# The S5 constants inside the first SwiGLU of a decoder block: whole pieces, part on VectorE, late zero stores, block sums in one tile per pair of rows

## The chip, the cores and the metric

The kernel runs on one core of a Trainium2 chip. The metric is the time of one execution in microseconds (us) of device time; the number that stands for a kernel is the median of its runs.

## What is computed

The reference is one layer of a decoder: half a SwiGLU, a mixer that joins sparse attention (8 heads) with an S5 state space layer, half a second SwiGLU, a gated per-layer input. The sequence has 512 rows, the model is 1024 wide, the hidden layer 2816 wide, everything in float32. The parts that matter here:

```python
h = h + 0.5 * swiglu(rmsnorm(h, norm_ffn1[i]), ffn1_w1[i], ffn1_w3[i], ffn1_w2[i])
z = rmsnorm(h, norm_mix[i]) @ w_in[i]
...
lam = lax.complex(a_re.astype(f32), a_im.astype(f32))
dt = jnp.exp(log_dt.astype(f32))[:, None]
a_bar = jnp.exp(lam * dt)
b_coef = (a_bar - 1.0) / lam
...
_, state = lax.associative_scan(combine, (a_seq, bu), axis=1)
```

The S5 layer has 32 groups of 16 channels with 64 complex states each. Its constants depend on the parameters alone (powers of `a_bar`, their products with the input and output matrices, cosines and sines), so the kernel can work them out while the first SwiGLU runs.

## The kernel before

**The first SwiGLU.** The hidden layer is cut into 22 tiles of 128 columns ("ups" 0 to 21), in four chunks of 6, 6, 5 and 5; after a chunk's ups comes its "down", which multiplies the chunk's hidden tiles back and adds to h. The first up of the next chunk stands ahead of each down. So up 12 is followed by down 1, then come ups 13 to 17, down 2, ups 18 to 21 and down 3. Each float32 product is made of three TensorE (PE) matmuls in a reduced float32 type: ScalarE (ACT) rounds a weight tile to `hi` (L164), VectorE (DVE) makes the rest `lo` (L166), and PE takes hi*hi, hi*lo and lo*hi. Weights come in units of 128x1024 (512 KB) through a ring of four buffers `raw`. Ups 0 to 13 use PSUM banks A and B and one 512-wide pass for each product; from up 14 on (`PLAIN`), `up_fast` forms a block product with seven instead of eight multiplications, for which DVE makes sums of weights (`s13`, `s24`, L342 to L351) and sums of the input.

**Sums of the input.** `renorm(k)` runs inside down 1, after every second of its eight output rows. It loads rows k and k+4 of x again (`xr`, L416, on SyncE's queue), scales them, splits them into xh and xl (L418 to L420), and makes the four sums of quarters in a tile `xt` (L427 to L430), which is split into `sh` and `sl` (L431, L432). Before, `sh` and `sl` are one tile each for all four k; `xt` shares its place with `s13` and `s24` by turns. These tiles lie where the S5 constants' pool was; a tile there has to wait until everything that used the place is done. In memory, `xt` of before overlaps `gt`.

**The S5 constants.** `s5_constants` is a generator: `ffn` takes the next piece of it behind an up, and `yield n` says that the next piece is not to come before up n. What is in a `with paced()` waits on GpSimd (POOL) for a small copy `step` that DVE makes at the end of each up (L407); POOL copies it to `seen` (L558). In order the generator makes: small tables on DVE; `ft`, eight times three POOL operations (L707 to L709); 32 transposes of it on PE (L715), copied to `fs` and stored to DRAM; `gt`, nine times three POOL operations (L728 multiply, L729 multiply into `ct`, L730 subtract), which takes the place of `ft` and so waits for the transposes; three stores of `gt` to DRAM (L731, L733); `kt`, 32 small matmuls of `b2` by `gt` (PE, bank D), eight stores of it interleaved with seven stores of zeros from the tile `zz` (L754); tables of cosines and sines `tcs` by doubling, j = 0 to 5 (L773 to L779), a multiply by a sign (L782) and two stores.

The instructions of each engine stand in one fixed list, in-order; a scheduler writes the lists at build time from the order of the code and its own estimates, apart from those that are pinned. An instruction that waits holds everything behind it on its engine. POOL, SyncE and ACT issue the DMAs.

Of the kernel before, what the change touches and what calls it, by code (L numbers as in the profile page):

```python
# [10 lines left out]
F32 = mybir.dt.float32  # L11
# [18 lines left out]
NG = 32  # L30
# [46 lines left out]
def block_kernel(ctx: ExitStack, tc: tile.TileContext, a: dict, out: bass.AP):  # L77
# [104 lines left out]
    class Norm:  # L182
# [25 lines left out]
        def quarter(self, r, c):  # L208
            ks, cs = slice(4 * r, 4 * r + 4), slice(256 * c, 256 * c + 256)
            return self.xh[:, ks, cs], self.xl[:, ks, cs]  # L210

# [5 lines left out]
    class Scaled(Norm):  # L217
# [13 lines left out]
        def spread(self, tmp, xpool, pool, pb):  # L231
# [22 lines left out]
            def combine(n, a, b, op):  # L254
                t = tmp().rearrange("p a (b c) -> p (a b) c", c=256)
                with tc.issue_after(self.last.ins):
                    for i in range(2):
                        V.tensor_tensor(t[:, 2 * i:2 * i + 2], a(i), b(i), op)
                hi = pool.tile([128, 4, 256], FR, name=f"sh{n}")
                lo = pool.tile([128, 4, 256], FR, name=f"sl{n}")  # L260
                S.copy(hi, t)
                V.tensor_tensor(lo, t, hi.bitcast(F32), OP.subtract)
                return (hi, lo), lambda i: t[:, 2 * i:2 * i + 2]

            q = {(r, c): (lambda i, r=r, c=c: quarter(r, c, i)) for r in range(2) for c in range(2)}
            self.t1, t1 = combine(1, q[0, 0], q[0, 1], OP.subtract)
            self.t2, t2 = combine(2, q[1, 1], t1, OP.add)
            self.t4, _ = combine(4, q[1, 0], t2, OP.subtract)
            self.t3, _ = combine(3, q[0, 1], q[1, 1], OP.subtract)

# [45 lines left out]
    def ffn(nrm, done, pools, plain, bg=None, first=None):  # L316
        wait = next(bg) if bg else None
        fast = bg is None
        with ExitStack() as fctx:
# [13 lines left out]
            def up_fast(f):  # L333
# [10 lines left out]
                u1 = split(s13.rearrange("p b c -> p (b c)"), kept=made.append)  # L344
                ah, al = (xp.tile([128, 512], FR, tag=n, name=n) for n in ("ah", "al"))
                with tc.issue_after(made[0].ins):
# [11 lines left out]
                def product(o, w, half, x, first):  # L358
                    for k in range(4):
                        sl = slice(512 * half + k * 128, 512 * half + (k + 1) * 128)  # L360
                        for i, (a_, b_) in enumerate(((0, 0), (0, 1), (1, 0))):
                            mm(o, w[a_][:, sl], x[b_][:, k], first and k + i == 0, k == 3 and i == 2,
                               skip_group_check=True)
# [22 lines left out]
                product(zx[:, lo], (ah, al), 0, nrm.quarter(1, 0), False)  # L386
                product(zy[:, lo], u2, 0, nrm.t2, False)
                product(zz[:, lo], u2, 1, nrm.quarter(1, 1), False)
# [20 lines left out]
            def renorm(k):  # L409
# [17 lines left out]
                V.tensor_tensor(t[:, 0], xs[0][:, c[0]], xs[0][:, c[1]], OP.subtract)  # L427
                V.tensor_tensor(t[:, 1], xs[1][:, c[1]], t[:, 0], OP.add)
                V.tensor_tensor(t[:, 2], xs[0][:, c[1]], xs[1][:, c[1]], OP.subtract)
# [122 lines left out]
    def s5_constants(sp, late_pool):  # L552
        yield 3
        if True:
# [157 lines left out]
            for g in range(0, NG, 4):  # L712
                p = bank("D")
                for j in range(4):
                    PE.transpose(p[:, j * 128:(j + 1) * 128], ft[:, g + j].rearrange("p s i -> p (s i)"), ident)  # L715
# [9 lines left out]
            for k in range(9):  # L725
                yield 8 + k // 3
                with paced():
                    G.tensor_tensor(gt[:, :, k, :], cp, bc(pr[:, k]), OP.mult)  # L728
                    G.tensor_tensor(ct, cx[:, 1], bc(pi[:, k]), OP.mult)  # L729
# [7 lines left out]
            for g in range(0, NG, 16):  # L737
# [12 lines left out]
            zz = late_pool.tile([128, 1, 112], F32, tag="zz", name="zz")  # L750
            G.memset(zz, 0.0)
# [28 lines left out]
            nc.gpsimd.dma_start(cd, tc_)  # L780
            for g in range(0, NG, 8):
                G.tensor_scalar(ts_[:, g:g + 8], ts_[:, g:g + 8], pos, None, OP.mult)  # L782
            nc.gpsimd.dma_start(sd, ts_)
# [22 lines left out]
    with ExitStack() as f1:  # L806
# [926 lines left out]
```

## Time and profile before

| | before |
|---|---|
| runs | 1086.9, 1090.21, 1092.48 us (median 1090.21) |
| profiled execution | 1088.84 us, span 1087.0 us |
| granted TensorE clock, mean | 0.987 |
| PE busy | 1040.2 us (96%) |
| DVE busy | 823.3 us (76%) |
| ACT, POOL busy | 492.0 us, 172.0 us |
| moved by DMA | 135.19 MB, 26.4 + 8.4 + 6.6% of the 16 engines' time |

"Busy" is time in which an engine has an instruction in work. A view of windows gives this for stretches of the span; in it, (x) counts instructions and PEclk is the share of TensorE's full clock that the chip granted there. A view of waits lists who waited for whom, as "waiter <- the one waited for: total us, times, longest us". The chain is the path followed back from the last instruction, each piece as "start, length, what". Groups give "busy us, mean ns of one". The end of a wait tells which dependency came last, and not what else would have come soon after. The first SwiGLU takes about the first 390 us of the span.

### The profile page before, as it was taken

The page shows a single profiled execution, that of the slowest core. Times are in us where ns is not written, and L with a number is a line of the kernel's source. Part 1 is how long each engine was busy: PE and PEld are TensorE (multiplying, and loading weights), DVE is VectorE, ACT ScalarE, POOL GpSimd, SP SyncE. Part 2 cuts the span into 40 slices and gives each one's busy share as a digit, 9 for nine tenths or more (in the row PEclk, how much of TensorE's full clock was granted, in tenths as well). Part 3 has the DMA queues.
Part 4 walks back from the last instruction along what each step waited for, and adds up shares of the span by engine and source line. Part 5 has one row for each costly group of instructions (what it writes and reads, how often), then busy time and mean ns, then how long its engine had stood idle before and what let it go on. Part 6 is the DMA issues. An engine that isn't in the chain of part 4 may idle for free.

```text
span 1087.0 us, 15732 instructions
## 1 busy us (share of the span) xinstructions
PE 1040.2 (96%) x6057; PEld 881.5 (81%) x6057; DVE 823.3 (76%) x1371; ACT 492.0 (45%) x852; POOL 172.0 (16%) x187
## 2 busy tenths in 40 slices
PE   8999999776998999998899999999999999999997
PEld 5887888665987988876668668899899899899886
DVE  5699456747978876788579887998589669677766
ACT  6322233313633553235677884655255345344542
POOL 2004648913059110010000000000000000000001
PEclk9999999888999999999999999999999999999999
DMA  7432325493434574876631003333333333323322
GB/s 249 158 97 97 97 82 183 122 190 106 122 111 115 145 248 127 226 253 185 187 118 59 1 21 125 107 117 117 97 98 117 100 94 117 97 97 117 106 88 78
DMA packets 52939, 135.19 MB, mean 124 GB/s; under 512 B 10817, under 2 KB 19105, under 8 KB 52865
## 3 DMA queue, kind: packets, MB, share of 16 engines
q10 hardware_dynamic: 26352, 90.77, 26.4%
q0 software_dynamic: 6416, 22.12, 8.4%
q1 hardware_dynamic: 20096, 21.31, 6.6%
q8 instruction: 47, 0.77, 0.3%
q14 instruction: 28, 0.22, 0.1%
HBM read 116.19 MB, written 17.83 MB: 123 GB/s over the span
## 4 chain that ended last, share of the span: by engine, by line
PE 75%; DVE 8%; DMA 7%; POOL 3%; issue 3%; ACT 2%; SPq 0%; ACTq 0%; DVEq 0%; POOLq 0%
PE ps_A L133 22%; PE ps_C L133 20%; PE ps_B L133 18%; PE ps_D L133 14%; DMA s5o<-gt 2%; DVE lo L166 2%; DMA xr<-in_xT 1%; POOL ct L729 1%; POOL gt L730 1%; DMA qf<-qd 1%; DMA qd<-r 1%; DMA h<-in_xT 1%; DMA kcd<-ra 1%; DVE h L525 0%; DVE el L1344 0%
## 5 line engine op out<-in xcount | busy, mean ns | idle before, releaser
L164 ACT CAST hi<-raw 128x1024 fp32r<-128x1024 f32 (+2 forms) x143 | 144.5, 1010 | 262.2 <-PE ps_C L133 96.3
L133 PE MATMUL ps_C<-hq,hi 128*128 128x512 f32 x704 | 217.9, 391 | 1.5 <-DVE h L525 1.3
L166 DVE TENSOR_TENSOR lo<-raw,hi 128x1024 fp32r<-128x1024 f32 (+2 forms) x143 | 179.7, 1258 | 43.7 <-ACT hi L164 42.7
L133 PEld LDWEIGHTS ps_C<-hq,hi 128*128 128x128 f32 x704 | 131.5, 189 | 29.6 <-ACT hi L164 1.7
L133 PE MATMUL ps_C<-hq,lo 128*128 128x512 f32 x352 | 136.8, 390 | 0.0
L133 PE MATMUL ps_A<-xh,hi 128*128 128x512 f32 (+1 forms) x352 | 126.6, 360 | 8.8 <-ACT xh L419 5.8
L133 PE MATMUL ps_A<-xh,lo 128*128 128x512 f32 (+1 forms) x352 | 124.1, 356 | 11.2 <-DVE lo L166 11.2
L133 PE MATMUL ps_A<-xl,hi 128*128 128x512 f32 (+1 forms) x352 | 125.7, 357 | 1.4 <-DVE xl L420 1.2
L164 ACT CAST hi<-s 128x1024 fp32r<-128x1024 f32 x56 | 59.0, 1053 | 99.2 <-PE ps_D L133 51.3
L166 DVE TENSOR_TENSOR lo<-s,hi 128x1024 fp32r<-128x1024 f32 x56 | 71.8, 1281 | 18.1 <-ACT hi L164 17.7
L133 PEld LDWEIGHTS ps_A<-xh,lo 128*128 128x128 f32 x352 | 67.6, 192 | 20.9 <-DVE lo L166 12.0
L133 PEld LDWEIGHTS ps_A<-xh,hi 128*128 128x128 f32 x352 | 67.5, 192 | 19.9 <-ACT xh L419 6.2
L133 PEld LDWEIGHTS ps_A<-xl,hi 128*128 128x128 f32 x352 | 67.4, 192 | 12.5 <-DVE xl L420 1.9
L133 PEld LDWEIGHTS ps_C<-hq,lo 128*128 128x128 f32 x352 | 66.2, 188 | 13.9
L525 DVE SCALAR_TENSOR_TENSOR h<-ps_C,h 128x512 f32<-128x512 f32 x64 | 43.9, 687 | 37.8 <-PE ps_C L133 37.5
L133 PE MATMUL ps_B<-sh,hi 128*128 128x256 f32 x224 | 63.1, 282 | 0.7 <-ACT hi L164 0.7
L133 PE MATMUL ps_B<-sh,lo 128*128 128x256 f32 x224 | 63.1, 282 | 0.6 <-DVE lo L166 0.6
L133 PE MATMUL ps_B<-xh,hi 128*128 128x512 f32 (+1 forms) x168 | 63.4, 378 | 0.0
L133 PE MATMUL ps_D<-sl,hi 128*128 128x256 f32 x224 | 63.0, 281 | 0.0
L133 PE MATMUL ps_B<-sl,hi 128*128 128x256 f32 x224 | 62.9, 281 | 0.0
L133 PE MATMUL ps_D<-sh,hi 128*128 128x256 f32 x224 | 62.8, 280 | 0.0
L133 PE MATMUL ps_D<-sh,lo 128*128 128x256 f32 x224 | 62.7, 280 | 0.0
(439 smaller groups left out, 2498.6 us busy)
## 6 DMA issues: line engine op xcount, KB each, us to landing
raw<-in_wpack ACTq DMA_DIRECT2D x168, 512.0 KB, 3.6
so<-s5o POOLq DMA_DIRECT2D x8, 768.0 KB, 6.0
si<-s5i POOLq DMA_DIRECT2D x8, 512.0 KB, 5.0
h<-in_xT SPq DMA_DIRECT2D x8, 256.0 KB, 4.7
s5i<-fs POOLq DMA_DIRECT2D x1, 2048.0 KB, 12.4
xr<-in_xT SPq DMA_DIRECT2D x8, 256.0 KB, 6.8
s5o<-gt POOLq DMA_DIRECT2D x1, 2048.0 KB, 13.1
s5o<-gt POOLq DMA_DIRECT2D x2, 1024.0 KB, 19.7
```

What stands on the lines that cost most here:

```text
L133: return PE.matmul(o, lhsT, rhs, start=start, stop=stop, **kw)
L164: p, q = S.copy(hi[:, c], raw[:, c]), None
L166: q = V.tensor_tensor(lo[:, c], raw[:, c], hi[:, c].bitcast(F32), OP.subtract)
L525: V.scalar_tensor_tensor(h[:, m, :], o[m], 0.5, h[:, m, :], OP.mult, OP.add)
L729: G.tensor_tensor(ct, cx[:, 1], bc(pi[:, k]), OP.mult)
L730: G.tensor_tensor(gt[:, :, k, :], gt[:, :, k, :], ct, OP.subtract)
```

## The change

1. The generator's pieces are larger: `ft` comes in two halves behind ups 5 and 6, all transposes and copies to `fs` in one piece behind up 7, `gt` in three pieces of three k behind ups 8, 9 and 10.
2. Of gt's nine first multiplies, six (k over 2) go to DVE, three stay on POOL.
3. The memset of `zz` and its seven stores stand ahead of `ft` and wait for a `step`; in before's lists, POOL issues them at the program's start.
4. `dd` takes the tag of `bt` and `ct`, so DVE's write of `dd` waits for POOL's last use of `ct`.
5. `yield 13` stands ahead of kt's eight stores, and each waits for a `step`, that of up 13. The tables j = 0 to 3 follow in the same piece, j = 4 and 5 from up 17 on.
6. `xt` goes to the pool of the sums under the tag `aa`, which `ah` and `al` also share as one tile later; `sh` and `sl` are one tile for each k. Of these, only the pair for k = 3 lies where `gt` lies; `s13` and `s24` lie there too.
7. The sign is put into six columns of `sn` by one small DVE operation ahead of the tables, in place of four POOL operations of 128x512 behind them.

```diff
             ft = sp.tile([128, NG, 8, 16], F32, tag="big0", name="ft")
             for s_ in range(8):
-                yield 5 + s_ // 4
+                if s_ % 4 == 0:
+                    yield 5 + s_ // 4
...
                 S.copy(fs[:, g:g + 4].rearrange("p g n -> p (g n)"), p)
-                if g % 8 == 4:
-                    yield 7 + g // 16
...
             for k in range(9):
-                yield 8 + k // 3
+                if k % 3 == 0:
+                    yield 8 + k // 3
+                if k > 2:
+                    V.tensor_tensor(gt[:, :, k, :], cp, bc(pr[:, k]), OP.mult)
                 with paced():
-                    G.tensor_tensor(gt[:, :, k, :], cp, bc(pr[:, k]), OP.mult)
+                    if k < 3:
+                        G.tensor_tensor(gt[:, :, k, :], cp, bc(pr[:, k]), OP.mult)
...
-            dd = sp.tile([16, NG, 16], F32, name="dd")
+            dd = sp.tile([16, NG, 16], F32, tag="bt", name="dd")
...
+            yield 13
             for s_ in range(8):
-                w = 128 - 16 * s_
-                nc.gpsimd.dma_start(md[16 * s_:16 * s_ + 16, :, 16 * s_:], kt[:, :, :w])
-                if s_:
-                    nc.gpsimd.dma_start(md[16 * s_:16 * s_ + 16, :, :16 * s_], zz[16 * s_:16 * s_ + 16, :, :16 * s_].to_broadcast([16, NG, 16 * s_]))
+                with paced():
+                    nc.gpsimd.dma_start(md[16 * s_:16 * s_ + 16, :, 16 * s_:], kt[:, :, :128 - 16 * s_])
...
+            snp = sn[:, 3:9]
+            V.tensor_scalar(snp, snp, pos, None, OP.mult)
             for j in range(6):
-                if j > 2:
+                if j > 3:
                     yield 17
...
-            for g in range(0, NG, 8):
-                G.tensor_scalar(ts_[:, g:g + 8], ts_[:, g:g + 8], pos, None, OP.mult)
...
-                if not k:
-                    nrm.ts = [xp.tile([128, 4, 4, 256], FR, name=n) for n in ("sh", "sl")]
-                    for i in range(4):
-                        setattr(nrm, f"t{i + 1}", tuple(t[:, :, i] for t in nrm.ts))
-                t = cp.tile([128, 4, 256], F32, tag=("s13", "s24")[k % 2], name="xt", bufs=1)
+                t = xp.tile([128, 4, 256], F32, tag="aa", name="xt")
+                sums = [xp.tile([128, 4, 256], FR, name=f"{n}{k}") for n in ("sh", "sl")]
+                for i in range(4):
+                    nrm.t[i].append([x[:, i] for x in sums])
```

In POOL's list, the stretch of `gt` from its middle to its end reads so before:

```order
L728 TENSOR_TENSOR gt<-cp,pr 128x32x16
L729 TENSOR_TENSOR ct<-cx,pi 128x512
L558 COPY seen<-step 128x1
L728 TENSOR_TENSOR gt<-cp,pr 128x32x16
L730 TENSOR_TENSOR gt<-gt,ct 128x32x16
L558 COPY seen<-step 128x1
L728 TENSOR_TENSOR gt<-cp,pr 128x32x16
L729 TENSOR_TENSOR ct<-cx,pi 128x512
```

The same stretch of POOL now (L738 and L739 are the old L729 and L730):

```order
L739 TENSOR_TENSOR gt<-gt,ct 128x32x16
L738 TENSOR_TENSOR ct<-cx,pi 128x512
L558 COPY seen<-step 128x1
L739 TENSOR_TENSOR gt<-gt,ct 128x32x16
L558 COPY seen<-step 128x1
L738 TENSOR_TENSOR ct<-cx,pi 128x512
L558 COPY seen<-step 128x1
L739 TENSOR_TENSOR gt<-gt,ct 128x32x16
```

POOL's first multiplies are gone from it; they stand on DVE, six in a row behind one up.

On DVE, the stretch of down 1 in which the sums of the input begin reads so before (`h<-ps_C` takes a finished row of down 1 from PSUM, `kt<-kt,dd` is the last step of kt):

```order
L525 SCALAR_TENSOR_TENSOR h<-ps_C,h 128x512
L420 TENSOR_TENSOR xl<-xr,xh 128x512
L749 TENSOR_TENSOR kt<-kt,dd 16x32x16
L166 TENSOR_TENSOR lo<-raw,hi 128x1024
L525 SCALAR_TENSOR_TENSOR h<-ps_C,h 128x512 x2
L166 TENSOR_TENSOR lo<-raw,hi 128x1024
L525 SCALAR_TENSOR_TENSOR h<-ps_C,h 128x512
L427 TENSOR_TENSOR xt<-xr 128x256
```

And now, from kt's last step on:

```order
L758 TENSOR_TENSOR kt<-kt,dd 16x32x16
L421 TENSOR_TENSOR xl<-xr,xh 128x512
L525 SCALAR_TENSOR_TENSOR h<-ps_C,h 128x512
L427 TENSOR_TENSOR xt<-xr 128x256
L166 TENSOR_TENSOR lo<-raw,hi 128x1024
L419 SCALAR_TENSOR_TENSOR xr<-xr,gains,rb 128x512 x2
L525 SCALAR_TENSOR_TENSOR h<-ps_C,h 128x512
L428 TENSOR_TENSOR xt<-xr,xt 128x256
```

The first `xt` stood behind the fifth row of down 1; now it stands behind the first, and the sums are spread over the rows.

The end of up 11 on DVE, with the new place of `dd`, reads now (`t_1584` belongs to up 11, `rb` is the row scale):

```order
L500 TENSOR_TENSOR t_1584<-ps_B,rb 128x512
L756 TENSOR_TENSOR dd<-ident,dk 16x512
L501 TENSOR_TENSOR t_1584<-t_1583,t_1584 128x512
L166 TENSOR_TENSOR lo<-raw,hi 128x1024
L329 CAST hq<-t_1584 128x512
L408 COPY step<-t_1584 128x1
```

Before, `dd` has a place of its own and stands near the head of DVE's list; now it stands between two steps of an up, and the `lo` behind it is that of the first weights of down 1.

More of the change, by code (lines that the diff above doesn't have):

```diff
@@ L208, in quarter @@
         def quarter(self, r, c):
-            ks, cs = slice(4 * r, 4 * r + 4), slice(256 * c, 256 * c + 256)
-            return self.xh[:, ks, cs], self.xl[:, ks, cs]
+            return [[x[:, 4 * r + k, 256 * c:256 * c + 256] for x in (self.xh, self.xl)] for k in range(4)]
         def finish(self, pin=False):
@@ L262, in combine @@
                 V.tensor_tensor(lo, t, hi.bitcast(F32), OP.subtract)
-                return (hi, lo), lambda i: t[:, 2 * i:2 * i + 2]
+                return [(hi[:, k], lo[:, k]) for k in range(4)], lambda i: t[:, 2 * i:2 * i + 2]
             q = {(r, c): (lambda i, r=r, c=c: quarter(r, c, i)) for r in range(2) for c in range(2)}
[L266 to L269, printed above, removed]
+            s1, t1 = combine(1, q[0, 0], q[0, 1], OP.subtract)
+            s2, t2 = combine(2, q[1, 1], t1, OP.add)
+            s4, _ = combine(4, q[1, 0], t2, OP.subtract)
+            s3, _ = combine(3, q[0, 1], q[1, 1], OP.subtract)
+            self.t = s1, s2, s3, s4
     def rsqrt_rows(parts, nb, pin=False, beside=None):
@@ L344, in up_fast @@
                 u1 = split(s13.rearrange("p b c -> p (b c)"), kept=made.append)
-                ah, al = (xp.tile([128, 512], FR, tag=n, name=n) for n in ("ah", "al"))
+                aa = xp.tile([128, 2, 512], FR, tag="aa", name="aa")
+                ah, al = aa[:, 0], aa[:, 1]
                 with tc.issue_after(made[0].ins):
@@ L361, in product @@
                         for i, (a_, b_) in enumerate(((0, 0), (0, 1), (1, 0))):
-                            mm(o, w[a_][:, sl], x[b_][:, k], first and k + i == 0, k == 3 and i == 2,
+                            mm(o, w[a_][:, sl], x[k][b_], first and k + i == 0, k == 3 and i == 2,
                                skip_group_check=True)
@@ L386, in up_fast @@
                 product(zx[:, lo], (ah, al), 0, nrm.quarter(1, 0), False)
-                product(zy[:, lo], u2, 0, nrm.t2, False)
+                product(zy[:, lo], u2, 0, nrm.t[1], False)
                 product(zz[:, lo], u2, 1, nrm.quarter(1, 1), False)
@@ L430, in renorm @@
                 V.tensor_tensor(t[:, 3], xs[1][:, c[0]], t[:, 1], OP.subtract)
-                S.copy(nrm.ts[0][:, k], t)
-                V.tensor_tensor(nrm.ts[1][:, k], t, nrm.ts[0][:, k].bitcast(F32), OP.subtract)
+                S.copy(sums[0], t)
+                V.tensor_tensor(sums[1], t, sums[0].bitcast(F32), OP.subtract)
             def up_pair():
@@ L700, in s5_constants @@
             V.tensor_scalar(psn, pi, neg, None, OP.mult)
+            zz = late_pool.tile([128, 1, 112], F32, tag="zz", name="zz")
+            with paced():
+                G.memset(zz, 0.0)
+            for s_ in range(1, 8):
+                nc.gpsimd.dma_start(md[16 * s_:16 * s_ + 16, :, :16 * s_],
+                                    zz[16 * s_:16 * s_ + 16, :, :16 * s_].to_broadcast([16, NG, 16 * s_]))
             ft = sp.tile([128, NG, 8, 16], F32, tag="big0", name="ft")
             for s_ in range(8):
-                yield 5 + s_ // 4
+                if s_ % 4 == 0:
+                    yield 5 + s_ // 4
                 e = 7 - s_
@@ L749, in s5_constants @@
             V.tensor_tensor(kt[:, :, 0:16], kt[:, :, 0:16], dd, OP.add)
-            zz = late_pool.tile([128, 1, 112], F32, tag="zz", name="zz")
-            G.memset(zz, 0.0)
+            yield 13
             for s_ in range(8):
-                w = 128 - 16 * s_
-                nc.gpsimd.dma_start(md[16 * s_:16 * s_ + 16, :, 16 * s_:], kt[:, :, :w])
-                if s_:
-                    nc.gpsimd.dma_start(md[16 * s_:16 * s_ + 16, :, :16 * s_], zz[16 * s_:16 * s_ + 16, :, :16 * s_].to_broadcast([16, NG, 16 * s_]))
+                with paced():
+                    nc.gpsimd.dma_start(md[16 * s_:16 * s_ + 16, :, 16 * s_:], kt[:, :, :128 - 16 * s_])
             tcs = late_pool.tile([128, 2, NG, 64], F32, tag="big1", name="tcs")
@@ L815, in combos @@
             s5c.close()
+            n1.t = [], [], [], []
             pool = fctx.enter_context(tc.tile_pool(name="sums", bufs=1, reuse_waits="tile"))
@@ L1396, in block_kernel @@
     ph = fp2.tile([128, 2, 512], FR, tag="s24", name="ph", bufs=1)
-    pls = [x2pool.tile([128, 512], FR, tag=n, name="pl") for n in ("ah", "al")]
+    pl = x2pool.tile([128, 2, 512], FR, tag="aa", name="pl")
+    pls = [pl[:, k] for k in range(2)]
     S.copy(ph, pp)
```

8 lines of the change are left out of this document (4 added, 4 removed).

## The prediction

> **What bounds the kernel now.** The page comes first. TensorE (PE) is busy for nearly the whole span, so only its idle time and slow clock can be won.
>
> ```profile
> PE 1040.2 (96%) x6057; PEld 881.5 (81%) x6057; DVE 823.3 (76%) x1371; ACT 492.0 (45%) x852; POOL 172.0 (16%) x187
> ```
>
> The windows place these losses (columns: window, length, busy PE, PEld, DVE, ACT, POOL, then PEclk, DMA share, GB/s).
>
> ```profile
> 0.00:24.00 24.00, 20.18 (x67) 13.22 (x68) 11.81 (x23) 13.75 (x24) 5.45 (x15) 0.93 0.84 262
> 130.00:150.00 20.00, 20.00 (x91) 16.56 (x90) 10.98 (x16) 4.57 (x6) 9.52 (x10) 1.00 0.33 96
> 150.00:168.00 18.00, 18.00 (x96) 15.24 (x95) 7.41 (x10) 8.53 (x13) 2.52 (x6) 1.00 0.26 84
> 190.00:212.00 22.00, 15.94 (x118) 12.48 (x118) 18.95 (x18) 7.29 (x11) 21.20 (x17) 0.84 0.34 106
> 212.00:237.00 25.00, 20.09 (x89) 16.32 (x87) 6.41 (x10) 4.90 (x7) 9.43 (x13) 0.96 0.94 223
> 237.00:270.00 33.00, 22.93 (x94) 18.16 (x94) 24.69 (x37) 10.91 (x14) 9.68 (x20) 0.82 0.49 90
> 270.00:300.00 30.00, 29.82 (x251) 29.82 (x252) 29.81 (x47) 17.69 (x30) 0.00 (x0) 1.00 0.46 141
> 300.00:330.00 30.00, 30.00 (x163) 25.96 (x162) 20.07 (x28) 10.03 (x15) 17.87 (x19) 1.00 0.35 106
> 330.00:348.00 18.00, 13.70 (x97) 12.73 (x96) 17.97 (x10) 4.78 (x8) 17.66 (x8) 0.99 0.30 72
> ```
>
> From 190 to 270 PE idles 6.06 + 4.91 + 10.07 = 21.0 us, and a granted clock of 0.84, 0.96 and 0.82 costs its 58.96 busy us about 2.6 + 0.8 + 4.1 = 7.5 more: 28.5 us in one stretch, and nearly none after it until 330, where 4.3 go. The start loses 3.8.
>
> The waits name who is late (waiter <- waited for: total, times, longest).
>
> ```profile
> PE ps_A L133 <- ACT xh L191: 2.4, 1, 2.4
> ...
> PE ps_D L133 <- POOL gt L730: 6.1, 1, 6.1
> ...
> PE ps_A L133 <- DVE lo L166: 6.9, 1, 6.9
> PE ps_A L133 <- ACT xh L419: 5.8, 1, 5.8
> ...
> PE ps_A L133 <- DVE lo L166: 4.3, 1, 4.3
> ...
> DVE xt L427 <- DMA s5o<-gt: 11.5, 1, 11.5
> ...
> SPq L416 <- DVE xt L429: 34.7, 2, 34.4
> ...
> POOL gt L728 <- PE ps_D L715: 4.2, 1, 4.2
> ```
>
> And the chain (start, length) joins them; PE's row at 270.18 is where it runs on again.
>
> ```profile
> 4.02 8.42 DMA h<-in_xT
> ...
> 134.92 5.44 PE ps_A L133 x24
> ...
> 166.22 0.87 PE ps_D L715 x8
> ...
> 213.98 21.60 DMA s5o<-gt
> 237.20 16.00 DMA xr<-in_xT
> ...
> 270.18 1.44 PE ps_B L133 x10
> ```
>
> Read as one story: PE waits 6.1 us for POOL's last `gt`; the stores of `gt` run until 213.98 + 21.60 = 235.6; DVE stands at the first `xt`, whose place `gt` holds, until then; SyncE's loads of `xr` wait 34.4 us for DVE's release, start at 237.2 and take 16.0 beside kt's stores; then DVE has to make up all sums at once, and PE waits 6.9 and 5.8.
>
> **The change part by part.** Places on PE are counted along its new list at 5.44/24 = 0.227 us a matmul from 134.92, those on DVE and POOL by the rows' means; both are estimates in the time of this trace.
>
> *Transposes in one piece, and when gt ends.* POOL's gt waits for the last transposes, 167.1 now. All 32 now begin with up 8, at 134.92, spread over 62 matmuls of it: at 0.227 us that is 14.1, and 4 x 0.87 = 3.5 for themselves, so 152.5. From there POOL works through these rows (group: busy us, mean ns):
>
> ```profile
> L730 POOL TENSOR_TENSOR gt<-gt,ct 128x512 f32<-128x512 f32 x9 | 15.0, 1671 | 0.3
> L729 POOL TENSOR_TENSOR ct<-cx,pi 128x512 f32<-128x512 f32 x9 | 14.1, 1572 | 0.4
> ...
> L728 POOL TENSOR_TENSOR gt<-cp,pr 128x512 f32<-128x512 f32 x9 | 9.6, 1081 | 4.2 <-PE ps_D L715 4.2
> L782 POOL TENSOR_SCALAR tcs<-tcs,sgn 128x512 f32<-128x512 f32 x4 | 8.3, 2077 | 0.1
> ```
>
> 15.0 + 14.1 + 3 x 1.08 for the multiplies left, and an estimated 3.5 for copies of `step` and fs's store: 36 us, so it ends at about 188.5. Before, its last row is
>
> ```profile
> 209.72 1.27 POOL L730 TENSOR_TENSOR gt<-gt,ct 128x512 f32<-128x512 f32 x1
> ```
>
> 22 us later. PE comes to kt's matmuls, now ahead of down 1, at about 193: the wait of 6.1 goes, with 4.5 us to spare.
>
> *Six multiplies on DVE.* The nearest rows are a DVE operation of that size in this stretch and the same with POOL silent:
>
> ```profile
> L501 DVE TENSOR_TENSOR t<-t,t 128x512 f32<-128x512 f32 x6 | 5.3, 878 | 0.6
> ...
> L350 DVE TENSOR_TENSOR s<-s,raw 128x512 f32<-128x512 f32 x2 | 1.4, 684 | 0.0
> ```
>
> So 6 x 0.68 to 0.88 = 4.1 to 5.3 us, where DVE has 9 of 20 and 10.6 of 18 us free. They follow the last transpose and end near 158; the weight tile behind them is needed near 166. Nothing; if the cover were gone, 5.
>
> *dd behind POOL.* DVE reaches it near 183 and stands until gt ends, 5.5 us. Behind it are `t_1584` and the first weights of down 1, which PE needs near 196.5: hidden, by about 5 us.
>
> *xt and the sums off gt's place.* The wait of 11.5 and the 34.4 of SyncE's queue go: pairs 0 to 2 don't touch gt's place. What is late next is gt's own traffic: its stores now run from about 190 to 212, where xr is loaded. On DVE the first tile on gt's place is then the `s13` of up 14, behind the fifth row of down 1, near 222: 10 us to spare. Loads under that traffic (median us to landing, in 205:237 and then on the page):
>
> ```profile
> raw<-in_wpack ACTq DMA_DIRECT2D x3, 512.0 KB, 9.6
> ...
> xr<-in_xT SPq DMA_DIRECT2D x1, 256.0 KB, 14.7
> ```
>
> ```profile
> raw<-in_wpack ACTq DMA_DIRECT2D x168, 512.0 KB, 3.6
> ...
> xr<-in_xT SPq DMA_DIRECT2D x8, 256.0 KB, 6.8
> ```
>
> A pair that meets it is 14.7 - 6.8 = 7.9 us late; two may: 0 to 15.8. SyncE's queue holds little else there, and DVE has some 36 us of work in 44 of PE, so I take 3. Of the 28.5 us, 25.5 are won.
>
> *kt's stores behind up 13.* The same rows: weight units land up to 6 us later while they run. The ring holds four units, two ups; 0 to 5, I take 1.
>
> *Tables.* Two things. The sign's 8.3 us on POOL go, and the end of the tables comes earlier against down 2 by j = 3 and this, some 14 us. In 330:348 POOL works beside a DVE that PE waits for (first fence), and DVE's rows grow against 280:300 (second):
>
> ```profile
> L166 DVE TENSOR_TENSOR lo<-s,hi 128x1024 fp32r<-128x1024 f32 x3 | 6.8, 2262 | 2.0 <-ACT hi L164 2.0
> L166 DVE TENSOR_TENSOR lo<-raw,hi 128x1024 fp32r<-128x1024 f32 x1 | 4.6, 4599 | 0.0
> ...
> L350 DVE TENSOR_TENSOR s<-s,raw 128x512 f32<-128x512 f32 x1 | 2.3, 2291 | 0.0
> ```
>
> ```profile
> L166 DVE TENSOR_TENSOR lo<-s,hi 128x1024 fp32r<-128x1024 f32 x5 | 6.1, 1219 | 0.1
> ```
>
> 3 x 1.04 + 3.38 + 1.61 = 8.1 us lost for 17.66 of POOL, 0.46 to one. The 4.3 us of PE shrink, I take 2.5 (0 to 4.3). Against that, j = 0 to 3 (9.7 us in 237:270 for j up to 2, and by the doubling sizes an estimated 6 for j = 3) moves from a time in which PE waited anyway to ups 14 to 17, where DVE is busy 29.81 of 30: 15.7 x 0.46 = 7.2 at most by that ratio. The memset ahead of them waits for kt's stores, so a part falls into down 2, where DVE has 10 of 30 free: I take 3.
>
> [...]
>
> *Zero stores.* They share the start with x and the first weights (0:30; packets, MB, share):
>
> ```profile
> q0 software_dynamic: 368, 0.92, 13.7%
> ```
>
> 13.7% of 30 us is 4.1 us of all 16 engines, a fifth of the 0.84 x 24 = 20.2 that they worked at the start; a fifth of the 8.42 us in which x lands is 1.7, and the slow clock of the first matmuls (0.93 of 24 us) starts and ends earlier: I take 2.5 of the 3.8 (1 to 3.8). Later, 0.92 MB meet a stage in which PE has no wait: 0.
>
> *Sum.* -25.5 - 2.5 - 2.5 + 1 + 3 = -26.5 on the profiled execution's 1088.84, so 1062.3. Its span is 1.8 us shorter than that, and the median of the runs 1.4 longer; I say 1062.5.
>
> **The rivals.** (a) gt's stores hold up the xr loads in full: two pairs, 15.8 in place of 3, with DVE in-order behind them: 1075. For it: 94% DMA share in 212:237. Against: the sums now have all of down 1.
>
> (b) The tables come one to one out of DVE and PE in ups 14 to 17: 15.7 in place of 3, 1075. For it: both engines full there. Against: 0.46 above. [...]
>
> (c) All losses go and nothing comes: 1088.84 - 28.5 - 4.3 - 2.5 = 1053.5.
>
> (d) The change moves the gap only: DVE's `s13` or the last sums wait for gt's stores as xt did, some 20 us: 1083, within 0.5% (5.4 us, about what a measurement of this kernel can tell).
>
> (e) Slower: POOL's gt ends no earlier than before, at 211, since DVE's multiplies and POOL's reads hinder each other, and DVE now stands at `dd` from 183 on with the weights of down 1 behind it. PE stops near 196.5 until 213, 16 us and 3 of slow clock where it lost 6.1: +12.9. gt's stores end at 235 again and catch `s13`, so the other 22 us stay; with tables at 7.2 and kt's stores at 5, less 2.5 at the start and 2.5 at down 2, that is +20: 1109. From a gt end past 193 it costs; past about 206, with 13 at `dd`, 9 at `s13` and 3 of clock, the gain is used up. Against it: 6.5 us of multiplies gone and a start 14.6 us earlier.
>
> **How the numbers follow.** Forecast 0.54 (its own range 1055 to 1070), (a) 0.17, (b) 0.12, (c) 0.05, (d) 0.06, (e) 0.06. The range 1052 to 1078 holds the first four: 0.88. Faster by over 0.5%: 0.88; within: 0.06; slower: 0.06.
>
> **What would show it.** Right: POOL's last gt subtract near 186 to 189 less the start's gain; no PE wait on it; no DVE wait on `s5o<-gt`; windows from 190 to 245 with PE near full at clock 1.0; PE's first up 14 product some 27 to 29 us earlier. Wrong: DVE standing over 8 us at `dd`, xr waits over 5 us in sum, PE losing over 5 us in ups 14 to 17 with POOL busy, or a gain at a place not named here.

## The result and the profile after

The changed kernel takes 1059.79 us (median of 4 runs, 1057.7 to 1061.31), the kernel before 1089.34 in the same comparison (median of 4, 1086.9 to 1092.48). The ratio is 0.9726, with a 95% interval from 0.9695 to 0.9757: 2.7% faster. The forecast was 1062.5, in a range from 1052 to 1078.

On the page, PE's share of the span is up by two points, and the chain has lost its stores of `gt`:

```profile
span 1058.5 us, 15706 instructions
...
PE 1034.6 (98%) x6057; PEld 878.3 (83%) x6057; DVE 823.8 (78%) x1378; ACT 492.0 (46%) x852; POOL 165.7 (16%) x186
...
PE 76%; POOL 7%; DVE 7%; issue 5%; DMA 4%; ACT 1%; SPq 0%; ACTq 0%; DVEq 0%; POOLq 0%
```

The work on PE is the same number of matmuls. What has gone is waiting and slow clock, and the windows of the changed kernel show where some is left (window, length, busy PE, PEld, DVE, ACT, POOL, then PEclk, DMA share, GB/s):

```profile
0.00:20.00 20.00, 18.45 (x71) 12.57 (x72) 12.58 (x24) 14.52 (x25) 1.49 (x7) 1.00 0.83 288
...
100.00:127.00 27.00, 24.44 (x101) 19.85 (x100) 12.75 (x13) 4.63 (x5) 25.72 (x19) 0.94 0.31 90
...
180.00:200.00 20.00, 20.00 (x145) 16.41 (x144) 12.54 (x21) 8.97 (x14) 9.22 (x9) 1.00 0.63 215
200.00:220.00 20.00, 15.50 (x65) 11.84 (x64) 14.30 (x22) 5.96 (x9) 0.00 (x0) 0.98 0.74 229
220.00:243.00 23.00, 23.00 (x98) 18.94 (x98) 20.49 (x31) 9.46 (x11) 0.00 (x0) 0.94 0.34 111
243.00:262.00 19.00, 19.00 (x163) 19.00 (x162) 17.23 (x26) 11.04 (x19) 13.00 (x24) 1.00 0.77 145
...
285.00:305.00 20.00, 19.22 (x87) 15.67 (x86) 15.25 (x18) 4.45 (x6) 16.87 (x13) 1.00 0.37 108
305.00:321.00 16.00, 15.57 (x103) 14.00 (x102) 14.05 (x10) 5.45 (x8) 12.24 (x6) 1.00 0.52 142
```

Before, the first 20 us and down 0 read:

```profile
0.00:20.00 20.00, 16.18 (x50) 10.02 (x51) 8.95 (x19) 9.75 (x18) 5.16 (x14) 0.91 0.89 274
...
100.00:127.00 27.00, 25.67 (x113) 20.94 (x113) 18.67 (x19) 5.26 (x5) 25.12 (x18) 1.00 0.27 85
```

Read against these and the prediction's rows: the first 20 us are at full clock; down 1, with 21.0 us idle and 7.5 of slow clock before, is left with 4.5 idle, 0.3 and 1.4 of clock (15.5 x 0.02, 23 x 0.06), 6.2 in all; the ups behind it lose nothing; down 2 and up 18 lose 1.2. In down 0, at 100 to 127, a hole has grown: 1.3 us idle have become 2.6, and 24.44 x 0.06 = 1.5 of slow clock come to them.

The waits say the same by name. PE no longer waits for `gt` or for `xh`, and at up 18 it waits 0.5 us in place of 4.3; what is left is in the main one kind, rows of h that DVE takes late (windows 100 to 160 and 160 to 250), and on DVE the two waits that the change adds or leaves:

```profile
PE ps_C L133 <- DVE h L525: 2.6, 1, 2.6
...
PE ps_C L133 <- DVE h L525: 4.5, 3, 2.7
...
DVE xr L419 <- DMA xr<-in_xT: 6.2, 5, 2.8
DVE dd L756 <- POOL gt L739: 5.5, 1, 5.5
```

Between 180 and 245, the loads of xr and the last two of gt's three stores (count, KB each, median us from issue to landing) are:

```profile
xr<-in_xT SPq DMA_DIRECT2D x8, 256.0 KB, 6.4
s5o<-gt POOLq DMA_DIRECT2D x2, 1024.0 KB, 22.1
```

POOL's list shows gt's end and its stores, 25 us ahead of before, and PE's row of kt's matmuls stands 4.6 us behind that end (POOL row, then PE row):

```profile
184.29 1.30 POOL L739 TENSOR_TENSOR gt<-gt,ct 128x512 f32<-128x512 f32 x1
185.89 1.68 POOL L740 DMA_DIRECT2D s5o<-gt  x1 [0.30 <-POOL gt L739]
...
190.17 1.94 PE L133 MATMUL ps_D<-gt,b 128*16 128x128 f32 x64
```

To place the gain, take DVE's rows that close a stage in both kernels: the fourth hidden tile after the first (last step of up 4), and the last row of down 0 and of down 3. Before:

```profile
72.65 0.68 DVE L330 TENSOR_TENSOR hq<-t,hq 128x512 fp32r<-128x512 f32 x1
...
125.21 0.69 DVE L525 SCALAR_TENSOR_TENSOR h<-ps_C,h 128x512 f32<-128x512 f32 x1 [2.86 <-PE ps_C L133]
...
407.59 0.69 DVE L525 SCALAR_TENSOR_TENSOR h<-ps_C,h 128x512 f32<-128x512 f32 x1
```

And after:

```profile
67.09 0.69 DVE L330 TENSOR_TENSOR hq<-t,hq 128x512 fp32r<-128x512 f32 x1
...
122.50 0.69 DVE L525 SCALAR_TENSOR_TENSOR h<-ps_C,h 128x512 f32<-128x512 f32 x1 [3.27 <-PE ps_C L133]
...
379.54 0.68 DVE L525 SCALAR_TENSOR_TENSOR h<-ps_C,h 128x512 f32<-128x512 f32 x1
```

So 5.6 us are won by up 4, 2.7 by the end of down 0, 28.1 by the end of the first SwiGLU. The spans differ by 28.5: the rest of the kernel is the same to 0.4 us.

### The profile page after: what moved, and what is told of

Read it like the earlier page. It is cut to its first block, busy times and chain, and to the rows that moved or that the text cites. A ratio compares the mean times of both kernels' runs of the same rounds, so it can differ in the third digit from the quotient of the medians.

```text
span 1058.5 us, 15706 instructions
## 1 busy us (share of the span) xinstructions
PE 1034.6 (98%) x6057; PEld 878.3 (83%) x6057; DVE 823.8 (78%) x1378; ACT 492.0 (46%) x852; POOL 165.7 (16%) x186
## 3 DMA queue, kind: packets, MB, share of 16 engines
q10 hardware_dynamic: 26352, 90.77, 26.5%
## 4 chain that ended last, share of the span: by engine, by line
PE 76%; POOL 7%; DVE 7%; issue 5%; DMA 4%; ACT 1%; SPq 0%; ACTq 0%; DVEq 0%; POOLq 0%
PE ps_A L133 23%; PE ps_C L133 21%; PE ps_B L133 17%; PE ps_D L133 15%; DMA xr<-in_xT 2%; POOL gt L739 1%; DVE lo L166 1%; POOL ft L716 1%; POOL bt L715 1%; POOL ft L714 1%; POOL ct L738 1%; DMA raw<-in_wpack 1%; DMA qd<-r 1%; POOL seen L558 0%; DVE el L1351 0%
## 5 line engine op out<-in xcount | busy, mean ns | idle before, releaser
L133 PE MATMUL ps_C<-hq,hi 128*128 128x512 f32 x704 | 220.3, 395 | 8.0 <-DVE h L525 7.8
L166 DVE TENSOR_TENSOR lo<-raw,hi 128x1024 fp32r<-128x1024 f32 (+2 forms) x143 | 174.9, 1224 | 42.4 <-ACT hi L164 41.3
L133 PE MATMUL ps_A<-xh,hi 128*128 128x512 f32 (+1 forms) x352 | 124.4, 353 | 0.4 <-ACT hi L164 0.4
## 6 DMA issues: line engine op xcount, KB each, us to landing
s5o<-gt POOLq DMA_DIRECT2D x2, 1024.0 KB, 22.1
```

The lines of the kernel that those rows point to most:

```text
L133: return PE.matmul(o, lhsT, rhs, start=start, stop=stop, **kw)
L166: q = V.tensor_tensor(lo[:, c], raw[:, c], hi[:, c].bitcast(F32), OP.subtract)
```

## The experiments

Three theories were to be told apart. Mine: two causes, the place of `xt` (part 6) and the late end of gt (parts 1, 2), and the start besides. The rivals: one of the two is the whole cause. Times are medians; a ratio is to the kernel before in the same comparison, with its 95% interval, and the changed kernel's is 0.9726.

**Late zero stores alone, on the kernel before.** The edit:

```diff
+            zz = late_pool.tile([128, 1, 112], F32, tag="zz", name="zz")
+            with paced():
+                G.memset(zz, 0.0)
+            for s_ in range(1, 8):
+                nc.gpsimd.dma_start(md[16 * s_:16 * s_ + 16, :, :16 * s_],
+                                    zz[16 * s_:16 * s_ + 16, :, :16 * s_].to_broadcast([16, NG, 16 * s_]))
...
-            zz = late_pool.tile([128, 1, 112], F32, tag="zz", name="zz")
-            G.memset(zz, 0.0)
...
-                if s_:
-                    nc.gpsimd.dma_start(md[16 * s_:16 * s_ + 16, :, :16 * s_], zz[16 * s_:16 * s_ + 16, :, :16 * s_].to_broadcast([16, NG, 16 * s_]))
```

> The kernel before with one part of the change alone: the seven stores of zeros wait for the step of up 5 instead of standing at the program's start. Theory A (the stores alone slow the start): the fourth hidden tile is done about 5.5 us earlier than before's 73.3 us, as in the changed kernel, the granted clock of the first 20 us goes to 1.0, and all of it reaches the end unless a later wait takes it: 1084 us. Theory B (the stores are a small part of it, as predicted, and the rest of the 5.5 comes from other moves on POOL and DVE in the first 70 us): 1.5 to 2.5 us at the same place, 1087 us. Theory C: the stages up to 270 us are set by gt and its stores, on whose way there is slack, so that the gain is used up by a longer wait there: 1089 us with a gain at the fourth tile.

1082.01 us, 0.9943 (0.9928 to 0.9959). Up 4 is done 5.4 us earlier, and the first 20 us run so:

```profile
0.00:20.00 20.00, 18.82 (x71) 13.25 (x72) 12.74 (x24) 14.72 (x26) 1.46 (x7) 1.00 0.84 290
```

Theory A. PE has 18.8 busy us there where it had 16.2, at clock 1.00 where it had 0.91: ACT waits 2.6 us for x there in place of 7.2, PE's stop of 2.4 us is gone, and the slow clock with it. All of it reached the end: the first SwiGLU ends 6.0 us sooner than before.

**The sums' tiles alone, on the kernel before,** part 6 of the change without the others:

```diff
-                t = cp.tile([128, 4, 256], F32, tag=("s13", "s24")[k % 2], name="xt", bufs=1)
+                t = xp.tile([128, 4, 256], F32, tag="aa", name="xt")
+                sums = [xp.tile([128, 4, 256], FR, name=f"{n}{k}") for n in ("sh", "sl")]
...
```

> The kernel before with only the sums' tiles changed: xt under aa beside gt's place, one pair of sh and sl for each k. gt still ends at 211 us and its stores at 235. Theory A (two causes of about the same size, the place of xt and the late end of gt): DVE's wait of 11.5 us for gt's stores at xt goes, PE's wait of 6.1 us for gt stays, s13 or the last pair still waits for the stores; 8 to 15 us faster than before, 1077 us. Theory B (the late end of gt is the whole cause): the wait moves from xt to s13 with the same length, under 4 us faster: 1087 us. Theory C (the place of xt is nearly the whole cause): 20 us or more faster, 1068 us.

1082.00 us, 0.9936 (0.9913 to 0.9958): 7.3 us, just under what theory A allowed and well over B. Its waits on PE and, last, on DVE:

```profile
PE ps_D L133 <- POOL gt L730: 6.1, 1, 6.1
PE ps_A L133 <- DVE lo L166: 4.1, 1, 4.1
...
DVE s L342 <- DMA s5o<-gt: 2.9, 1, 2.9
```

DVE's 11.5 us at xt are gone, and 2.9 of them come back where the first `s13` needs the same place; the wait for gt itself is untouched.

**The sums' tiles put back, on the changed kernel** (the same lines, reversed).

> The changed kernel with only the sums' tiles put back: xt on gt's place by turns with s13 and s24, one sh and one sl for all k. gt ends at 185 us and its stores land near 210. Theory A: the first xt, early in down 1, waits on DVE for the stores from about 200 to 210, the loads of xr behind it are late, and PE loses 8 to 14 us: 1070 us. Theory B (the early end of gt is enough by itself): the stores are home before DVE needs the place, within 3 us of the changed kernel: 1061 us. Theory C: the waits of before come back in full in the stage from 212 to 270 (21 us): 1080 us.

1066.43 us, 0.9797 (0.9769 to 0.9826): 6.6 us slower than the changed kernel, neither B nor quite A. DVE and PE:

```profile
DVE xt L427 <- DMA s5o<-gt: 12.5, 1, 12.5
...
PE ps_C L133 <- DVE h L525: 10.8, 1, 10.8
```

The wait at xt is back in full although gt ends 25 us earlier: xt now stands early in down 1. So part 6 is worth 7.3 us without the others and 6.6 with them, a separate cause. With it and the zero stores taken off, the rest of the change (pieces, multiplies, pacing, sign) has to account for 1089.3 - 1066.4 less the zero stores' 6 to 7, some 16 us.

**kt's stores at once, on the changed kernel.**

```diff
-            yield 13
             for s_ in range(8):
-                with paced():
-                    nc.gpsimd.dma_start(md[...], kt[:, :, :128 - 16 * s_])
+                nc.gpsimd.dma_start(md[...], kt[:, :, :128 - 16 * s_])
```

> The changed kernel with kt's eight stores right behind kt, in the stage in which gt's stores run and xr is loaded, and not behind up 13; the tables j = 0 to 3 follow them and so come earlier too. Theory A (pacing the stores is worth something, the traffic of kt hinders the loads of xr): DVE's waits for xr grow from 6 us to 12 or more, PE loses 4 to 8 us before up 14 and wins back 3 to 5 in ups 14 to 17, from which kt's stores and a part of the tables are gone: 1062 us. Theory B (the stores are harmless among xr's loads): only the gain in ups 14 to 17 is left, 4 to 5 us faster than the changed kernel: 1055 us. Theory C: xr meets them in full, 8 us for each of two pairs: 1070 us.

1063.74 us, 0.9766 (0.9733 to 0.9798), 4 us slower than the changed kernel. The two intervals overlap, but in the trace the first SwiGLU ends 4.9 us later. The waits on DVE and PE, then the loads of xr between 180 and 245 (count, KB each, median us to landing):

```profile
DVE xr L419 <- DMA xr<-in_xT: 11.7, 4, 5.0
...
PE ps_C L133 <- DVE h L525: 9.6, 3, 8.1
```

```profile
xr<-in_xT SPq DMA_DIRECT2D x8, 256.0 KB, 11.7
```

The traffic of kt nearly doubles the loads' time (11.7 against 6.4), as theory A had it; the gain it expected in ups 14 to 17 isn't there, since nothing is lost there (below).

**All tables behind up 17, on the changed kernel.**

```diff
-                if j > 3:
+                if j == 0 or j > 3:
                     yield 17
```

> The changed kernel with all tables (j = 0 to 5) behind up 17; kt's stores stay behind up 13. From the third to the last of ups 14 to 17 the changed kernel needs 29.1 us for three ups, the kernel before 23.7. Theory A (POOL's tables slow DVE there, kt's stores hardly): the three ups take 24 to 26 us; the tables end some 14 us later, at about 330, and slow DVE at up 18 as before, 3 to 5 us: 1059 to 1062 us. Theory B (kt's stores and late weights slow them, not the tables): the three ups stay at 28 to 29 us, and the later tables cost besides: 1063 to 1066 us.

1065.83 us, 0.9787 (0.9765 to 0.9810), 6 us slower. B's time, but neither theory's reason. I had read "three ups in 29.1 against 23.7 us" from DVE's last step of each up, and DVE's steps trail PE by a varying amount: in the changed kernel the last steps of ups 14 to 17 begin 12.1, 9.3 and 7.8 us apart. PE's own rows say that nothing was lost: 163 matmuls in 19 us at 243 to 262, 8.6 a us, against 251 in 30, 8.4 a us, in the full stage before. What the later tables cost is at up 18:

```profile
PE ps_A L133 <- ACT p L368: 4.8, 1, 4.8
```

**gt's nine multiplies on POOL, on the changed kernel.**

```diff
-                if k > 2:
-                    V.tensor_tensor(gt[:, :, k, :], cp, bc(pr[:, k]), OP.mult)
                 with paced():
-                    if k < 3:
-                        G.tensor_tensor(gt[:, :, k, :], cp, bc(pr[:, k]), OP.mult)
+                    G.tensor_tensor(gt[:, :, k, :], cp, bc(pr[:, k]), OP.mult)
```

> The changed kernel with all nine first multiplies of gt on POOL. Six by 1.1 us make gt end at about 192 in place of 185.6; PE comes to kt's matmuls at 190.2, and DVE stands at dd for 12 us in place of 5.5. Theory A (slack 4.6 us, the rest costs): PE waits 2 us there, the weights of down 1 come 1 to 2 us late, gt's stores end at 217 and still ahead of s13: 2 to 4 us slower than the changed kernel, 1063 us. Theory B (the wait of dd carries over): DVE's 12 us delay the loads and the sums by the same, 8 us or more slower: 1069 us. Theory C (the six multiplies cost DVE as much as they save POOL): within 1 us, 1060 us.

1061.68 us, 0.9748 (0.9734 to 0.9763): 2 us slower, a difference within the intervals. In the trace gt ends at 191.0 in place of 185.6. DVE stands at `dd` 6.2 us instead of the 12 expected, since in this list `dd` comes behind more of up 11's work, and PE doesn't wait at kt. The later stores seem to cost at the loads: DVE waits 8.2 us for xr, PE 8.9 for h in down 1, and the first SwiGLU ends 4.1 us later; behind it this execution is 2.9 us shorter than the changed kernel's, which nothing here explains. Theory A's size, at another place than it said, and not clear of noise in the time.

**The smaller pieces, on the changed kernel.**

```diff
-                if s_ % 4 == 0:
-                    yield 5 + s_ // 4
+                yield 5 + s_ // 4
...
+                if g % 8 == 4:
+                    yield 7 + g // 16
...
-                if k % 3 == 0:
-                    yield 8 + k // 3
+                yield 8 + k // 3
```

> The changed kernel with the smaller pieces of before: transposes spread over two ups, gt's and ft's parts one by one. gt then starts about 10 us later. Theory A (the whole pieces pull gt forward, and with dd behind it the delay costs): gt ends near 196 to 200, PE waits 6 to 9 us at kt, DVE stands at dd 16 us or more, gt's stores end near 222 and catch s13 or the last loads: 1068 to 1075 us. Theory B (POOL has idle time enough and takes up the delay): 1060 to 1063 us.

1072.35 us, 0.9850 (0.9835 to 0.9864): 12.6 us slower, theory A. gt ends at 200.4, and PE's waits are

```profile
PE ps_D L133 <- POOL gt L739: 6.0, 1, 6.0
PE ps_C L133 <- DVE h L525: 4.2, 1, 4.2
PE ps_D L133 <- DVE sl L432: 2.8, 1, 2.8
```

The first is before's wait for gt, to a tenth. Of the parts that a run has taken alone, the larger pieces are the largest. The hole in down 0 is smaller here and at full clock, but not gone:

```profile
100.00:127.00 27.00, 25.24 (x112) 20.61 (x111) 14.85 (x15) 5.81 (x6) 17.82 (x13) 1.00 0.30 98
```

**ft held for psn, on the changed kernel,** for the hole in down 0. Just ahead of it, POOL runs eight multiplies in a row and DVE's small products stretch (timeline of the changed kernel; the 128x128 products take 0.28 us while POOL is silent):

```profile
93.06 10.28 POOL L714 TENSOR_TENSOR ft<-b,pr 128x512 f32<-128x512 f32 x8 [0.65 <-DVE b L693]
...
92.90 0.28 DVE L660 TENSOR_TENSOR pr<-u,u 128x128 f32<-128x128 f32 x1
...
94.59 1.15 DVE L661 TENSOR_TENSOR u<-pr,pi 128x128 f32<-128x128 f32 x1
95.66 1.15 DVE L662 TENSOR_TENSOR u<-pi,pr 128x128 f32<-128x128 f32 x1
```

```diff
+            spn = late_pool.tile([128, 1], F32, tag="seen", name="seen")
+            seen_psn = G.tensor_copy(spn, psn[:, 0, 0:1]).ins
...
-                with paced():
+                with paced(), tc.issue_after(seen_psn) if s_ > 2 else nullcontext():
                     G.tensor_tensor(ft[:, :, s_, :], b2[:, 0], bc(pr[:, e]), OP.mult)
+                with paced():
                     G.tensor_tensor(bt, b2[:, 1], bc(psn[:, e]), OP.mult)
```

> The changed kernel with ft's eight first multiplies held on POOL until DVE has made psn, so that they don't run beside DVE's last small products ahead of the third row of down 0. Theory A (the 2.8 us that the changed kernel loses in down 0, where PE waits 2.6 us for h, come from POOL's run of eight multiplies): DVE reaches that row 3 to 4 us earlier, PE's wait goes to 0 to 1 us; ft ends at about 130, just ahead of the transposes: 2 to 3.5 us faster than the changed kernel, 1057 us. Theory B (the loss has another cause): the wait stays, 1060 us. Theory C: ft comes too late for the transposes, PE waits 2 to 4 us there instead: 1061 us.

1063.33 us, 0.9779 (0.9745 to 0.9813), slower by 3.5. With POOL silent beside DVE's small products the hole is gone: PE is busy 27.00 of 27 us in that window, and down 0 ends 4.3 us earlier. But the copy of `psn` stands ahead of everything else in POOL's list: POOL waits 67 us for it and issues the zero stores only behind it, 4.6 us in the middle of ft. With a start 5.3 us later, these stores and sixteen copies of `step` between its operations, ft ends at 138.6 instead of 126.9 and gt at 195.4, and PE waits 5.1 us for gt.

**ft behind one copy of psn, on the changed kernel,** with that copy behind the zero stores and without the copies of `step`:

```diff
-                nc.gpsimd.dma_start(md[16 * s_:16 * s_ + 16, :, :16 * s_],
+                zs = nc.gpsimd.dma_start(md[16 * s_:16 * s_ + 16, :, :16 * s_],
...
+            spn = late_pool.tile([128, 1], F32, tag="seen", name="seen")
+            with tc.issue_after(zs.ins):
+                seen_psn = G.tensor_copy(spn, psn[:, 0, 0:1]).ins
...
-                with paced():
+                with tc.issue_after(seen_psn):
                     G.tensor_tensor(ft[:, :, s_, :], b2[:, 0], bc(pr[:, e]), OP.mult)
```

> The changed kernel with ft on POOL behind one copy of psn, without copies of step, so that POOL is silent while DVE makes its last small products ahead of the third row of down 0, and its work behind that is short. Theory A (POOL's run of eight multiplies is the cause of the loss in down 0, and what the held kernel lost later was ft's late end by its sixteen copies): PE's wait of 2.6 us for h goes, ft ends near 127 as in the changed kernel, gt within 2 us of 186, nothing is given back: 3 to 4 us faster than the changed kernel, 1056 us. Theory B (PE that is earlier by 4 us only meets the later waits, for gt and for the xr loads, which stand still): within 1 us of the changed kernel, 1060 us. Theory C (slower lists elsewhere): 1062 us or more.

1059.06 us, 0.9745 (0.9726 to 0.9764): the changed kernel's time. Theory B. The hole is gone and down 0 ends 3.4 us earlier, ft ends at 132.0 and gt at 187.0, and a good part is given back in down 1:

```profile
180.00:200.00 20.00, 17.38 (x132) 13.95 (x131) 11.04 (x18) 8.72 (x13) 10.65 (x11) 0.99 0.63 189
200.00:220.00 20.00, 17.05 (x61) 13.25 (x62) 15.33 (x25) 6.46 (x9) 0.00 (x0) 0.84 0.80 247
```

PE is sooner at down 1, but gt is not. DVE stands at `dd` 7.4 us for it and takes the first row of h at 199.1, as in the changed kernel (198.7), so PE waits 2.6 us for that row in the first window and runs at 0.84 in the second. Idle time and slow clock from 180 to 243 come to 8.7 us against 6.2: 2.5 of the 3.4 us are given back there, and the first SwiGLU ends 1.2 us earlier.

**No gt stores among the loads, on the changed kernel.**

```diff
-            nc.gpsimd.dma_start(gd, gt[:, :, 1:9, :].rearrange("p g k o -> p g (k o)"))
...
             nc.gpsimd.dma_start(sd, ts_)
+            for to in (gd, gs):
+                for c_ in (0, 64):
+                    nc.gpsimd.dma_start(to[:, :, c_:c_ + 64], tc_)
```

> The changed kernel without gt's stores where they are: other data of the same size (the table of cosines) goes to their place in DRAM behind the tables, so gt's part of the result is left out. Nothing is stored while xr is loaded. Theory A (gt's stores slow the xr loads, and DVE's 6.2 us of waiting for xr and PE's 4.5 us of waiting for h in down 1 come from it): xr lands in 3 to 4 us in place of 6.4, DVE waits under 1.5 us for it, PE loses 4 to 6 us less between 200 and 243: 1055 us. Theory B (the loads are late because their tiles come free late): DVE's wait and PE's loss stay within 1.5 us: 1059 us.

1057.34 us (1054.55 to 1061.65), 0.9739 (0.9712 to 0.9765); its profiled execution took 1054.55. DVE's wait, and the loads between 180 and 245:

```profile
DVE xr L419 <- DMA xr<-in_xT: 1.5, 1, 1.5
```

```profile
xr<-in_xT SPq DMA_DIRECT2D x8, 256.0 KB, 3.1
```

Theory A in down 1: PE is busy 43.0 of the 43 us from 200 to 243, at clock 1.00, and loses 0.5 us ahead of them. The stores set behind the tables took part of it back behind up 18, where PE waits 2.8 us for ACT and slows down:

```profile
325.00:345.00 20.00, 17.20 (x132) 16.85 (x131) 15.32 (x23) 10.67 (x19) 1.67 (x1) 0.91 0.85 227
```

So its median shows 2.5 of the 6.2 us, and its ratio nothing: the first SwiGLU ends 4.8 us earlier in the trace, whose execution was the shortest of the four.

**gt's stores in two halves, on the changed kernel.** The first half goes out when POOL has made it:

```diff
+                if k == 4:
+                    nc.sync.dma_start(gd[:, :, 0:64], gt[:, :, 1:5, :].rearrange("p g k o -> p g (k o)"))
...
-            nc.gpsimd.dma_start(gd, gt[:, :, 1:9, :].rearrange("p g k o -> p g (k o)"))
+            nc.gpsimd.dma_start(gd[:, :, 64:128], gt[:, :, 5:9, :].rearrange("p g k o -> p g (k o)"))
...
```

> The changed kernel with gt's stores in two halves: k = 1 to 4 go out on SyncE's queue as soon as POOL has made them, near 170 us, and k = 5 to 8 behind the end of gt on POOL's queue, so that half of the traffic is gone before xr is loaded. Its rows in DRAM are half as long (256 bytes). Without any of these stores PE lost 6 us less between 200 and 243. Theory A (the traffic counts by its bytes among the loads): half of the loss goes, xr lands in about 5 us, 3 us faster than the changed kernel: 1056.5 us. Theory B (short rows cost as much time as long ones, and the first half runs into the weights' loads): no gain or a loss of up to 4 us, 1060 to 1064 us.

1051.98 us (1051.33 to 1053.28), 0.9659 (0.9645 to 0.9672): 7.8 us faster than the changed kernel (7.3 by the ratios), more than theory A's 3, and the best version here. Its windows, DVE's wait, and the transfers between 180 and 245:

```profile
100.00:127.00 27.00, 24.44 (x108) 19.95 (x107) 14.65 (x14) 5.79 (x6) 25.82 (x19) 1.00 0.31 98
...
180.00:200.00 20.00, 20.00 (x145) 16.41 (x144) 13.08 (x20) 8.84 (x13) 7.87 (x7) 1.00 0.96 270
200.00:220.00 20.00, 20.00 (x90) 16.45 (x89) 19.65 (x31) 9.84 (x12) 0.00 (x0) 1.00 0.65 201
```

```profile
DVE xr L419 <- DMA xr<-in_xT: 0.3, 1, 0.3
```

```profile
xr<-in_xT SPq DMA_DIRECT2D x8, 256.0 KB, 3.7
...
s5o<-gt POOLq DMA_DIRECT2D x2, 512.0 KB, 15.1
```

Not half but all of the loss in down 1 (6.2 us) is gone. The second half is home at about 203 in place of 211; the first two loads of xr still take 6.9 us beside it, but the median of all eight falls from 6.4 to 3.7. Of the rest of the gain, 1.4 us come before gt's stores, where down 0 runs at clock 1.00 with the same hole; no run shows that the halves bring this. The edit changes the time of the first half and its queue together, and no run parts the two.

**Both: halves, and ft behind one copy of psn.**

> The same with ft behind one copy of psn, which won 4 us in down 0 and gave them back in down 1. Theory A: what was given back went to the xr loads beside gt's stores, so with half of them gone 2 us of the 4 stay: 1054 us. Theory B: it went to the late end of gt (DVE at dd, PE at kt), which the halves don't change: as the kernel with halves alone, within 1 us.

1055.00 us, 0.9692 (0.9673 to 0.9711), 3 us slower than the halves alone. Neither theory: A's 1054 us was reckoned from an expected 1056.5 for the halves, and meant a gain. Down 0 has no hole (27.00 busy us of 27, against 24.44 with the halves alone), but PE waits once for a row of h at the head of down 1 and once at up 18:

```profile
PE ps_C L133 <- DVE h L525: 2.0, 1, 2.0
...
PE ps_A L133 <- DVE lo L166: 2.9, 1, 2.9
```

The first is theory B's in kind: DVE stands at `dd` 7.4 us, where it stood 5.5 with the halves alone, and takes that row at 197.9 as without the hold (197.4). From 305 to 325 PE is busy 16.95 of 20 us at clock 0.91 for the second, against 19.57 at 1.00 with the halves alone: the 2.6 us won in down 0 are more than given back. Why this list meets the wait at up 18 wasn't tried.

## Why the prediction was right

The time and the sign came out, and so did the mechanism of the largest term. Four of the terms were off, in both directions, and their errors nearly cancel: that the sum came within 3 us is in part luck.

- **Down 1.** Predicted 25.5 of 28.5 us won, measured 28.5 - 6.2 = 22.3. The steps hold. PE's last transposes end at 149.9 and gt at 185.6; predicted were 152.5 and 188.5 in the time of before, which is 149.8 and 185.8 when the 2.7 us won by the end of down 0 are taken off. PE had 4.6 us to spare at kt (4.5), DVE stood 5.5 us at `dd` (5.5) at no cost to PE, and no DVE wait on gt's stores is left. The six multiplies took DVE 6.8 us beside POOL, more than the 4.1 to 5.3 predicted, and PE didn't wait for it. The mis-sized term is the loads beside gt's stores: taken as 3 us, it cost 6.2. That is rival (a) in part, and without these stores all but 0.5 us of it is gone. Two of the prediction's own signs tell the same: DVE's waits for xr add up to 6.2 us, over the 5 that it named as a sign of being wrong, and PE is busy only 15.5 of 20 us from 200 to 220.
- **The start.** 2.5 predicted from the stores' share of the transfers; 5.4 measured by that part alone, 5.6 in the changed kernel. I took 2.5 out of the 3.8 us of idle time and left the slow clock out of the 3.8. By the rows, 2.3 us of idle time went and 20.18 x 0.07 = 1.4 of clock; for the other 1.9 of the 5.6 no row here names a cause.
- **Down 0.** Nothing predicted; 2.8 us lost (2.6 + 1.5 against 1.3 before). I costed ft's larger pieces only by what they bring to the transposes. POOL's multiplies in a row stretch DVE's small products ahead of a row of h; without them there the hole is gone, as the two runs with ft held show. The size of the pieces is only a part of it: with the smaller ones 1.8 us stay idle, and before, six multiplies in a row stretched the same products, to 1.15 and 1.14 us. The 1.5 us of slow clock are missing in other kernels with the same wait (last section). The stretching in the changed kernel's trace is from 0.28 us to 1.15, about one POOL multiply (10.28 / 8 = 1.29). I had taken the mean of 0.46 and only for the tables.
- **Tables and kt's stores.** 3 + 1 predicted as cost in ups 14 to 17, none measured: PE is busy 19.00 of 19 us from 243 to 262 and 23.00 of 23 from 262 to 285, at clock 1.00. Rival (b) fell: no run shows its one to one. DVE's rows there do stretch: `lo<-raw` takes a mean of 1.60 us from 262 to 285, where POOL makes the tables, against 1.22 from 243 to 262, where it copies `step` and issues kt's stores.
- **Down 2 and up 18.** 2.5 predicted, 4.4 - 1.2 = 3.2 won.

In sum: 5.6 - 2.8 + 22.3 + 3.2 = 28.3, where the first SwiGLU ended 28.1 sooner. The forecast's 26.5 was met because the start won 3 more and the tables cost 4 less, while down 0 and the loads took 6. One sign missed: PE's first product of up 14 comes 19.4 us earlier (262.1 to 242.7), not 27 to 29. Some twelve matmuls of up 13 that stood behind it before now stand ahead of it (2.7 us), a part of before's waits came only after it, and over the whole stretch 25.1 us were won, not 28. The single-part runs give the sizes: pieces 12.6, sums 6.6 to 7.3, zero stores 6 to 7, pacing of kt's stores 4 to 5, six multiplies about 2, which is within the noise. They add up to more than the whole, so the parts overlap.

## What to carry to other kernels

Where a buffer's release runs through a store, look at three things apart: when the store starts, what else is placed on the buffer, and which loads its traffic meets; each was worth several us here, and splitting the store so that half of it leaves early was worth more (7.8 us) than any further shift of the compute that was tried. Work moved off the critical path can be cheap in sum and dear at the place where it runs (in down 0, DVE products of 0.28 us took 1.15 beside POOL's multiplies): look at which small operations of the other engine stand beside it. And read a stage's rate from the engine that bounds it, not from when another engine finishes a step.

## What of the hardware was not expected

- A wait of 2.6 us in down 0 came with a slow clock in some profiled executions and not in others. Over the window from 100 to 127 the changed kernel shows 0.94, the kernel with halves and the one without gt's stores among the loads 1.00, with the same wait and the same 24.44 busy us, one execution each. What decides between the two was not shown.
- A load of xr (256 KB) took a median of 3.1 us without gt's stores, 6.4 with them, 11.7 with gt's and kt's.
- Halving the rows of gt in DRAM from 512 to 256 bytes cost less than the rest of that edit won: the kernel is 7.8 us faster. The last 2 MB of the halves landed 15.1 us after their issue, the 4 MB of the whole 22.1: about a third more by the byte (7.6 against 5.5 us for each MB), an estimate that counts the time of issue in both and the other traffic beside them.
